# Attention with a score product for the row maxima and a second one with keys on partitions, in place of transposed probabilities

## The chip, the cores and the metric

The kernel runs on one core of one Trainium2 chip. The metric is the device time of one execution in microseconds (us). The core's engines run side by side and wait for each other by semaphores: TensorE (PE; PEld is its loading of weights), VectorE (DVE), ScalarE (ACT), GpSimd (POOL), and SyncE (SP), which issues most transfers.

## What is computed

One program holds two blocks over 512 latent tokens of width 1024 and 256 context tokens. The first block (retention, neighbourhood and memory attention, a mixture of experts) is untouched by the change. The second block is two transformer layers, each with modulation, an attention of three kinds, and a gated feed-forward part. The attention of every head is

```
def _sdpa(q, k, v, scale):
    s = einsum('qd,kd->qk', q, k) * scale
    p = softmax(s, axis=-1)
    return einsum('qk,kd->qd', p, v)
```

in float32. A layer has 20 heads: 4 latent heads (query and key width 96), 8 differential ones (width 32, in four pairs whose outputs are subtracted and normalized), and 8 grouped ones (width 64; four heads share keys and values). Values are 64 wide. In layer 0 the 512 latent queries see all 768 keys, and the 256 context queries see the 256 context keys; in layer 1 only the latent queries are needed.

## The kernel before, in words

Numbers that need float32 accuracy go through TensorE as float32r, each as a high and a low part that add up (`split`, line 88: ScalarE rounds the high part, VectorE subtracts). Queries and keys of a latent head are split in two, and a score is three products of 96 rows: high by high, high by low, low by high. A differential head stacks its parts on 96 rows and needs one product. A grouped head stacks the query's two parts over twice the key's high part (128 rows, `k1`) and adds the query's high part by the key's low part (64 rows, `k2`).

`pipeline` (line 1867) runs over the 20 heads. For each head, `scores` (line 1888) takes the query tiles of 128 one by one: the products fill a PSUM tile of 128 queries by 768 keys (`sn`, line 1899; two such tiles exist, of two banks each), VectorE takes the negated maximum of each row (line 1905), ScalarE writes the exponentials `pn` with the maximum as bias and sums the rows on the way (line 1908). The two context tiles share one tile (lines 1913, 1919); line 1921 takes the reciprocals of the sums (`srec`).

`turned` (line 1924) then brings the keys onto partitions: per part of 128 keys by 512 queries (in layer 0 also one of 2 x 128 keys by 256 context queries) four float32 transposes `tp` on TensorE (line 131), and a split: by ScalarE from PSUM and VectorE (line 92), or, for the parts marked in `SPLITS` (line 1864), a copy by ScalarE (line 1940), a cast by VectorE (line 1941), and a subtraction on GpSimd (line 1942). `products` (line 1948) multiplies them with the values: the values, high and low side by side (`vp`, 128 columns), are the weights, and the 512 probabilities move past, high part and low part in turn (line 1957). ScalarE copies the result `oT` (line 1961), `fold` (line 1966) turns it back and adds the two halves by one float32 product per query tile (line 1970), and VectorE multiplies with the reciprocal into the merged rows `yB` (line 2001; line 1817 for the differential heads).

The order is written out in the loop of `pipeline`: a step of head u's `turned`, the products of parts that are more than `LAG` = 5 behind (line 1984), a step of head u+1's `scores`, and one step of preparing head u+2 (line 1992): its rows are loaded, split on VectorE and GpSimd (`dqst`, `gqst`), and turned by float32r transposes (line 129). Of PSUM's eight banks the two score tiles take four, `tp` three, `pv` one (line 1238). After the last head the merged rows are transposed (`trp`) for the output projection.

Of the kernel before, what the change touches and what calls it, by code (L numbers as in the profile page):

```python
# [23 lines left out]
# columns of the vector pack, in blocks of 128 features  # L24
# [8 lines left out]
# groups of 256 columns of the second block's input projection: name, first column  # L33
# [4 lines left out]
class Kern:  # L38
# [15 lines left out]
    def W(self, ap, n=2048, k=None, steps=1, pin=False, eng=None):  # L54
        """Weight chunk [128, n] of float32 from DRAM as an exact pair of float32r tiles."""
        key = ap.tensor.name, ap.offset
        if key in self.early:
            return self.early.pop(key)
        return self.pair(self.raw(ap, n), n, k, steps, pin, eng)

    def ahead(self, *chunks):
        """Loads weight chunks (name, index, k) before their use; W finds them then."""
        for name, at, k in chunks:
            ap = self.i[name][at]
            key = ap.tensor.name, ap.offset
            self.early[key] = self.W(ap, k=k)
# [6 lines left out]
    def pair(self, raw, n=2048, k=None, steps=1, pin=False, eng=None):  # L73
        """pin: not before what the engines have to do first, though it may seem ready."""
# [12 lines left out]
    def split(self, hi, lo, src, scale=None, bias=None):  # L87
        """hi + lo = src (times scale), both float32r."""
# [15 lines left out]
    def psum(self, mm, big=0, words=1024, own=()):  # L104
        """Banks of PSUM: mm of one bank, big of several."""
# [16 lines left out]
    def rows6(self, name, dtype=F):  # L122
        """[128, 6, 1024]: six tiles of rows, or what else takes their place."""
# [53 lines left out]
    def transpose_rows(self, rows, nt, dst, evac):  # L177
        """rows: list of [128, 1024] tiles; evac(kt, t0, n, psum [128, n*128])."""
# [25 lines left out]
    # =====================================================================  # L204
# [70 lines left out]
    def first_norm(self, t):  # L275
        """Norms the row tiles from t on that share a step: 0, 1, or 2 and 3."""
# [41 lines left out]
    def proj_a(self, g, evac):  # L318
        """Columns on partitions: out[128 columns, 512 tokens]."""
# [17 lines left out]
    def retention(self):  # L337
# [6 lines left out]
        y = rp.tile([128, 4, 1024], F, name="y")              # [tok, tile, 4 heads of 256]  # L344
# [3 lines left out]
        def queries(c):  # L348
            """q and k of the heads 2c, 2c + 1: [128, hi or lo, head, tok]"""
# [34 lines left out]
        def scores(hd):  # L384
            # decay by the distance of the tokens: E[p, i - 128 j + 384] for tile j of the keys
# [15 lines left out]
        def outputs(hd):  # L401
# [4 lines left out]
            for i in range(4):  # L406
# [6 lines left out]
                # group norm over the head's 256 values  # L413
# [9 lines left out]
        # log sigmoid of the decays: min(x, 0) - log1p(exp(-|x|)), log1p by its atanh series  # L423
# [41 lines left out]
        # silu of the gate projection  # L465
# [64 lines left out]
        # per query column qq of a tile, the 32 columns of its key window, for the three tile types  # L530
        # (window starts 16, 8 and 0 columns before the tile): [qq, qr, h, type, 256]
# [6 lines left out]
    def neighbourhood(self):  # L538
# [19 lines left out]
        starts = (256, 192, 64, 0)               # key windows of the query tiles 3, 2, 1, 0  # L558
# [42 lines left out]
    def exps(self, out, s, m, scale):  # L601
        """out = exp(scale * (s - max)) for two tiles of queries [128, 2, 256]; returns 1 / row sums."""
# [47 lines left out]
    def memory_rows(self):  # L650
        """Normed rows of the memory."""
# [14 lines left out]
    def memory_keys(self, rows):  # L666
        """Keys and values of the memory."""
# [63 lines left out]
    def b1_out(self, *stages):  # L731
        """stages: what follows for each tile of rows; the sums of squares of its parts are in self.xss."""
# [39 lines left out]
    # =====================================================================  # L772
    def moe(self):
# [21 lines left out]
        # normed rows, to DRAM for the gathers and transposed for the router  # L795
# [37 lines left out]
        # group: maximum of the softmax, first one on ties  # L833
# [1418 lines left out]
```

## Time and profile before

| | |
|---|---|
| three runs | 3068.51, 3056.35, 3059.96 us, median 3059.96 |
| profiled execution | span 3055.9 us, so the median lies 4.1 us above it |
| TensorE busy | 95% of the span |
| its weight loads | 81% |
| VectorE, ScalarE, GpSimd busy | 58%, 42%, 16% |
| attention of layer 0 | about 1258 to 1548 us of the span |
| attention of layer 1 | about 2364 to 2607 us |

Matmuls are pipelined, so the time that one shows is longer than the distance from its start to the next one's; what a product costs in a row of others is read from starts. A group "x4" in a timeline is four instructions on end. Where a float32 product with a narrow moving side runs, the trace holds two records for it.

### The profile page before, as it was taken

How to read it: one execution, taken by the hardware profiler on the slowest of the kernel's cores; microseconds unless marked ns; L12 is line 12 of the kernel's file. 1: busy time of each engine (PE TensorE's matmuls, PEld its weight loads, DVE VectorE, ACT ScalarE, POOL GpSimd, SP SyncE). 2: the span in 40 equal slices, each digit the busy share in tenths (PEclk: the TensorE clock that was granted, in tenths of full speed). 3: DMA queues.
4: the chain of work that ended last, by engine and by line, in shares of the span. 5: the costliest groups of instructions: out<-in, count | busy, mean ns of one | idle time of the engine just before them, and what ended most of it. 6: DMA issues, size and time to landing. Idle time of an engine off the chain costs nothing. (4 is left out here: it accounts for less than half of the span.)

```text
span 3055.9 us, 44719 instructions
## 1 busy us (share of the span) xinstructions
PE 2907.7 (95%) x17896; PEld 2473.1 (81%) x17896; DVE 1784.5 (58%) x3187; ACT 1296.3 (42%) x2275; POOL 483.3 (16%) x478
## 2 busy tenths in 40 slices
PE   8999999999899979899998999999898999899998
PEld 6997777679788869787688888888798776788887
DVE  6652254346688876788747242434665886644445
ACT  3232243324577754597645121211342876432222
POOL 2200010001110042255312000000310543100001
PEclk9999999999899989999999999999999999899999
DMA  5443464446799862510023121212143300322221
GB/s 197 153 140 138 143 234 152 183 155 242 267 392 378 312 225 75 179 27 19 1 90 128 59 71 54 78 48 83 62 138 98 96 20 1 125 110 96 97 97 69
DMA packets 130084, 399.78 MB, mean 131 GB/s; under 512 B 62199, under 2 KB 74887, under 8 KB 93128
## 3 DMA queue, kind: packets, MB, share of 16 engines
q1 hardware_dynamic: 116206, 350.04, 31.9%
q0 software_dynamic: 13520, 46.55, 4.6%
q8 instruction: 143, 2.34, 0.3%
q14 instruction: 71, 0.58, 0.1%
q10 hardware_dynamic: 144, 0.26, 0.0%
HBM read 356.64 MB, written 39.39 MB: 130 GB/s over the span
## 5 line engine op out<-in xcount | busy, mean ns | idle before, releaser
L82 DVE TENSOR_TENSOR wlo<-raw,whi 128x2048 fp32r<-128x2048 f32 (+2 forms) x195 | 419.3, 2153 | 280.2 <-ACT whi L81 279.7
L81 ACT ACTIVATE whi<-raw 128x2048 fp32r<-128x2048 f32 (+2 forms) x203 | 351.9, 1739 | 490.9 <-PE fd L101 132.2
L99 PE MATMUL fg<-hT,whi 128*128 128x512 f32 (+1 forms) x1120 | 389.1, 348 | 2.1 <-ACT hT L1374 2.1
L100 PE MATMUL fg<-hT,whi 128*128 128x512 f32 (+1 forms) x1120 | 389.7, 348 | 1.2 <-POOL hT L1376 1.2
L101 PE MATMUL fg<-hT,wlo 128*128 128x512 f32 (+1 forms) x1120 | 389.2, 348 | 0.0
L100 PEld LDWEIGHTS fg<-hT,whi 128*128 128x128 f32 x1120 | 213.7, 191 | 31.0 <-POOL hT L1376 1.7
L99 PEld LDWEIGHTS fg<-hT,whi 128*128 128x128 f32 x1120 | 212.1, 190 | 31.9 <-ACT hT L1374 2.5
L101 PEld LDWEIGHTS fg<-hT,wlo 128*128 128x128 f32 x1120 | 212.0, 189 | 29.0
L1942 POOL TENSOR_TENSOR pelo<-pe,pehi 128x512 fp32r<-128x512 f32 x140 | 180.7, 1292 | 233.5 <-DVE pehi L1941 227.1
L2104 DVE TENSOR_TENSOR sg<-sg,fg 128x512 f32<-128x512 f32 (+1 forms) x70 | 40.1, 572 | 295.0 <-PE fg L101 295.0
L101 PE MATMUL fd<-whi,hl 128*128 128x512 f32 x440 | 174.9, 397 | 0.0
L1905 DVE TENSOR_REDUCE smx<-sn 128x1 f32<-128x768 f32 x160 | 152.3, 952 | 38.2 <-PE sn L1899 37.7
L100 PE MATMUL fd<-wlo,hh 128*128 128x512 f32 x440 | 174.6, 397 | 0.0
L99 PE MATMUL fd<-whi,hh 128*128 128x512 f32 x440 | 174.1, 396 | 0.0
L2080 POOL TENSOR_TENSOR acc<-acc,gt 128x512 f32<-128x512 f32 x20 | 30.7, 1536 | 867.9 <-ACT sqj L164 867.9
L2075 DVE TENSOR_TENSOR acc<-acc,fd 128x512 f32<-128x512 f32 x180 | 120.7, 685 | 71.9 <-PE fd L101 71.9
L131 PE MATMUL tp<-ident,pn 128*128 128x128 f32 x960 | 151.8, 278 | 2.6 <-DVE pelo L92 1.8
L1908 ACT ACTIVATE pn<-sn,smx 128x768 f32<-128x768 f32 x160 | 143.5, 902 | 12.0 <-DVE smx L1905 6.8
L99 PE MATMUL eg<-whi,xt 128*96 128x256 f32 x512 | 146.5, 286 | 0.0
L100 PE MATMUL eg<-wlo,xt 128*96 128x256 f32 x512 | 144.6, 282 | 0.9 <-DVE wlo L82 0.9
L82 DVE TENSOR_TENSOR wlo<-rawx,whi 128x2048 fp32r<-128x2048 f32 x58 | 132.9, 2292 | 20.9 <-ACT whi L81 20.8
L101 PE MATMUL eg<-whi,xt 128*96 128x256 f32 x512 | 144.3, 282 | 0.0
(661 smaller groups left out, 7755.8 us busy)
## 6 DMA issues: line engine op xcount, KB each, us to landing
raw<-in_w_in SPq DMA_DIRECT2D x53, 1024.0 KB, 5.0
raw<-in_w_ada SPq DMA_DIRECT2D x48, 1024.0 KB, 5.1
raw<-in_f_gate SPq DMA_DIRECT2D x22, 1024.0 KB, 4.8
raw<-in_f_up SPq DMA_DIRECT2D x22, 1024.0 KB, 4.8
raw<-in_f_down SPq DMA_DIRECT2D x22, 1024.0 KB, 4.8
rawx<-in_e_gate SPq DMA_DIRECT2D x19, 1024.0 KB, 14.2
rawx<-in_e_up SPq DMA_DIRECT2D x19, 1024.0 KB, 8.9
rawx<-in_e_down SPq DMA_DIRECT2D x18, 1024.0 KB, 8.3
```

Of the source, the lines that this page charges most:

```text
L81: keep(nc.scalar.activation(hi[:, c], raw[:, c], AF.Copy))
L82: keep((eng or nc.vector).tensor_tensor(lo[:, c], raw[:, c], hi[:, c].bitcast(F), op=OP.subtract))
L99: t.matmul(ps, lh, rh, start=first, stop=False)
L100: t.matmul(ps, lh, rl, start=False, stop=False)
L101: t.matmul(ps, ll, rh, start=False, stop=last)
L131: self.nc.tensor.transpose(out, in_, self.ident[:k, :k])
L1905: nc.vector.tensor_reduce(m[:, t:t + 1], p[:, :768], axis=AX.X, op=OP.max, negate=True)
L1908: nc.scalar.activation(P[t], p[:, :768], AF.Exp, bias=m[:, t:t + 1], accum_out=su[:, t:t + 1])
L1942: nc.gpsimd.tensor_tensor(el, e, eh.bitcast(F), op=OP.subtract)
L2075: nc.vector.tensor_tensor(acc[:, t, cs], acc[:, t, cs], p, op=OP.add)
L2080: nc.gpsimd.tensor_tensor(acc[:, t, cs], acc[:, t, cs], gt[t // 4][:, cs], op=OP.mult)
L2104: nc.vector.tensor_tensor(sg, sg, pp[1], op=OP.mult)
```

## The change

Each head now has two score products. `maxima` (in place of `scores`) makes a first one, with queries on partitions and with the first pass alone (high by high for latent heads, all of it for differential ones, the 128-row pass for grouped ones); VectorE writes the negated row maxima into a column of a padded tile `mz`, small products with the identity turn that tile, and ScalarE copies the one row of maxima under the queries' rows (`late`). The keys get a row of ones at the same place, so that `exps` can make a second product, with keys on partitions and 256 queries moving, from which the maxima are already subtracted: 97 rows in place of 96, and 65 in place of 64. ScalarE's exponential of it is already in the layout that the product with the values wants. It is used as it is, in float32, for parts 2 and 5 of the differential and grouped heads (`plain`), and otherwise split: the high part by ScalarE or VectorE (`HIGH`), the low part on GpSimd.

In `products` the probabilities are now the weights (128 x 128), and the values move: 130 columns of [low, high, ones] for the high part, 66 of [high, ones] for the low part. Query tiles come out on partitions and the column of ones gives the sums, so `turned`, the accumulating of sums in the exponential, and `fold` go. Each pair of query tiles ends by a reciprocal, a copy, an addition, and a multiplication that moves from VectorE to GpSimd. There is one score tile for the maxima in place of two, two banks each are for `st`, `pv` and `tp`, and `LAG` is 4. A few memsets on GpSimd write the ones, and a copy on VectorE makes the second query tile of grouped heads.

```diff
-                with self.pool("l_at") as ap, self.psum(1, 2, own=dict(pv=1, tp=3)):
+                with self.pool("l_at") as ap, self.psum(1, 1, own=dict(st=2, pv=2, tp=2)):
...
-        nc.vector.tensor_copy(v[:, :, :64], r)
-        nc.gpsimd.tensor_tensor(v[:, :, 64:], r, v[:, :, :64].bitcast(F), op=OP.subtract)
-        return v
+        nc.vector.tensor_copy(v[:, :, 64:128], r[:, :, :64])
+        nc.gpsimd.tensor_tensor(v[:, :, :64], r[:, :, :64], v[:, :, 64:128].bitcast(F), op=OP.subtract)
+        nc.gpsimd.memset(v[:, :, 128:130].bitcast(F), 1.0)
+        nc.gpsimd.memset(r[:, :, 64:66], 1.0)
+        return v, r
...
-        return [(hi[0], hi[1], 96), (hi[0], lo[1], 96), (lo[0], hi[1], 96)], v
+        return dict(first=(hi[0], hi[1], 96), row=96, late=hi[0], v=v, plain=(),
+                    passes=[(hi[1], hi[0], 97), (lo[1], hi[0], 96), (hi[1], lo[0], 96)])
...
-            return [(q, k, 96)], v
+            return dict(first=(q, k, 96), row=96, late=q, passes=[(k, q, 97)], v=v, plain=(2, 5))
...
-            return [(q1, T1, 128), (q1, T2, 64)], v
+            return dict(first=(q1, T1, 128), row=64, late=q2, passes=[(T1, q1, 128), (T2, q2, 65)], v=v, plain=(2, 5))
...
-    SPLITS = (1, 0, 1, 0, 1, 0, 1)
-    LAG = 5
+    HIGH = (1, 0, 0, 1, 0, 0, 1)
+    LAG = 4
...
-        groups = [(0, 4, 0)] + ([(4, 2, 4)] if nq > 4 else [])
+        groups = [(0, 0, 6), (2, 0, 6)] + ([(4, 4, 6)] if nq > 4 else [])
...
+        def maxima(u):
...
             for t in range(4):
                 p = self.big("sn")
-                mms(p[:, :512], t, 0, 512)
-                mms(p[:, 512:768], t, 512, 768)
-                nc.vector.tensor_reduce(m[:, t:t + 1], p[:, :768], axis=AX.X, op=OP.max, negate=True)
-                P[t] = ap.tile([128, 768], F, name="pn", bufs=6)
+                qs = slice(t * 128, t * 128 + 128)
+                for a, b in ((0, 512), (512, 768)):
+                    nc.tensor.matmul(p[:, a:b], q[:rows, qs], k[:rows, a:b], start=True, stop=True)
+                nc.vector.tensor_reduce(mz[:, t, row:row + 1], p[:, :768], axis=AX.X, op=OP.max, negate=True)
                 yield
-                nc.scalar.activation(P[t], p[:, :768], AF.Exp, bias=m[:, t:t + 1], accum_out=su[:, t:t + 1])
...
+            for t0 in range(0, nq, 4):
+                n = min(4, nq - t0)
+                p = self.mm("tp")
+                for t in range(n):
+                    nc.tensor.matmul(p[:row + 1, t * 128:t * 128 + 128], mz[:, t0 + t, :row + 1], self.identr, start=True, stop=True)
+                nc.scalar.activation(late[row:row + 1, t0 * 128:(t0 + n) * 128], p[row:row + 1, :n * 128], AF.Copy)
+                yield
+        def exps(u):
...
+                    for a in range(2):
+                        ks = slice((k + a) * 128, (k + a) * 128 + 128)
+                        for j, (kT, qT, rows) in enumerate(passes):
+                            nc.tensor.matmul(p[:, a * 256:a * 256 + 256], kT[:rows, ks], qT[:rows, qs], start=j == 0,
+                                             stop=j == len(passes) - 1)
+                    if i in plain:
+                        e, eh, el = ap.tile([128, 512], F, name="pf", bufs=3), None, None
+                        nc.scalar.activation(e, p, AF.Exp)
                     else:
-                        self.split(eh, el, p)
+                        e = ap.tile([128, 512], F, name="pe", bufs=4)
+                        nc.scalar.activation(e, p, AF.Exp)
+                        eh, el = self.pairs8[0]
+                        self.pairs8.append(self.pairs8.pop(0))
+                        if self.HIGH[i]:
+                            nc.scalar.activation(eh, e, AF.Copy)
+                        else:
+                            nc.vector.tensor_scalar(eh, e, 1.0, None, op0=OP.mult)
+                        nc.gpsimd.tensor_tensor(el, e, eh.bitcast(F), op=OP.subtract)
...
             if k == k0:
                 self.pv = self.mm("pv")
-            p = self.pv[:, :N]
-            for a in range(512 // N):
-                for e in (eh, el):
-                    nc.tensor.matmul(p, v[:, k + a], e[:, a * N:a * N + N], start=k == k0 and a == 0 and e is eh,
-                                     stop=k + a == 5 and e is el)
...
+                    if eh is None:
+                        add(pv[:, t, 64:130], e[:, c], vf[:, k + a, :66], first, last)
+                    else:
+                        add(pv[:, t], eh[:, c], v[:, k + a], first, False)
+                        add(pv[:, t, 64:130], el[:, c], v[:, k + a, 64:130], False, last)
+            if k + 2 < k1:
                 return
-            folds.append([1, u, o, rec])
...
+            rec = self.small.tile([128, 2, 1], F, name="srec")
+            nc.vector.reciprocal(rec, pv[:, :, 128:129])
+            o = ap.tile([128, 2, 64], F, name="oS", bufs=3)
+            nc.scalar.activation(o, pv[:, :, :64], AF.Copy)
+            nc.vector.tensor_tensor(o, o, pv[:, :, 64:128], op=OP.add)
+            units[u][1](t0, rec.to_broadcast([128, 2, 64]), o)
...
     def scaled(self, yB, c, nq):
-        def ev(rec, p):
-            self.nc.vector.tensor_tensor(yB[:, :nq, c:c + 64], p, rec, op=OP.mult)
+        def ev(t0, rec, o):
+            self.nc.gpsimd.tensor_tensor(yB[:, t0:t0 + 2, c:c + 64], o, rec, op=OP.mult)
```

On TensorE, a stretch among the grouped heads of layer 0 stands so in the program before (`sn` are score tiles, `gkT` and `gqT` turned keys and queries, `tp` transposes, `pn` exponentials, `pv` the products with the values, `pehi` and `pelo` the split probabilities; behind the arrow the operands, with the moving shape):

```order
L1899 MATMUL sn<-gkT_14252,gqT_14710 128x512
L1899 MATMUL sn<-gkT_14295,gqT_14710 128x512
L1899 MATMUL sn<-gkT_14252,gqT_14710 128x256
L1899 MATMUL sn<-gkT_14295,gqT_14710 128x256
L129 MATMUL tp<-identr,gk_14838 128x128 x4
L131 MATMUL tp<-ident,pn 128x128 x4
L1957 MATMUL pv<-pehi,vp 128x512
L1957 MATMUL pv<-pelo,vp 128x512
```

And so, at the like place, in the changed program (`st` are scores with keys on partitions; the tile 15319 is the low part of the next group's keys):

```order
L1919 MATMUL sn<-gkT_14617,gqT_15159 128x512
L1919 MATMUL sn<-gkT_14617,gqT_15159 128x256
L129 MATMUL tp<-identr,gk_15319 65x128 x4
L1947 MATMUL st<-gqT_14979,gkT_14617 128x256
L1947 MATMUL st<-gqT_14978,gkT_14676 128x256
L1947 MATMUL st<-gqT_14979,gkT_14617 128x256
L1947 MATMUL st<-gqT_14978,gkT_14676 128x256
L1975 MATMUL pv<-vp,pehi 128x130
L1975 MATMUL pv<-vp,pelo 128x66
L1975 MATMUL pv<-vp,pehi 128x130
L1975 MATMUL pv<-vp,pelo 128x66
```

The second pass of the scores left the product for the maxima, the transposes of `pn` gave way to scores, and two wide products with the values became eight narrow ones per part (two pairs of them are shown).

On GpSimd, at the start of the grouped heads, the program before has (`gqst` is the split of a query, `vp` that of the values):

```order
L1840 TENSOR_TENSOR gqst<-gqr,gqst 128x6x64
L1942 TENSOR_TENSOR pelo<-pe,pehi 128x512 x3
L1840 TENSOR_TENSOR gqst<-gqr,gqst 128x6x64
L1942 TENSOR_TENSOR pelo<-pe,pehi 128x512
L1840 TENSOR_TENSOR gqst<-gqr,gqst 128x6x64
L1721 TENSOR_TENSOR vp<-vr,vp 128x6x64
```

The changed program has there (`yB` are merged rows, `oS` the output before its scaling, `do` the second output of a differential pair):

```order
L1838 TENSOR_TENSOR do_14558<-yB 128x384
L1860 TENSOR_TENSOR gqst<-gqr,gqst 128x6x64
L1829 TENSOR_TENSOR yB<-oS,srec 128x2x64
L1961 TENSOR_TENSOR pelo<-pe,pehi 128x512
L1860 TENSOR_TENSOR gqst<-gqr,gqst 128x6x64
L1961 TENSOR_TENSOR pelo<-pe,pehi 128x512 x2
L1829 TENSOR_TENSOR yB<-oS,srec 128x2x64
L1961 TENSOR_TENSOR pelo<-pe,pehi 128x512
```

The scaling of the outputs came in between GpSimd's subtractions, and there are more of these: 196 in both layers, where 140 stood.

## Rows read from the trace of the kernel before

**Rows 1.** Windows, latent/differential/grouped heads, layers 0, 1: us, busy (count), clock, DMA, GB/s:

```profile
1272.25:1313.12 40.87, 37.78 (x261) 33.03 (x260) 33.27 (x58) 33.34 (x77) 21.28 (x19) 1.00 0.41 121
1313.12:1407.57 94.45, 88.03 (x627) 75.49 (x626) 85.91 (x138) 85.83 (x202) 57.91 (x53) 1.00 0.12 26
1407.57:1532.72 125.15, 124.33 (x670) 87.21 (x669) 90.14 (x150) 82.28 (x189) 48.73 (x40) 1.00 0.03 6
2376.68:2409.90 33.22, 30.99 (x201) 25.74 (x199) 29.35 (x50) 26.87 (x57) 18.66 (x16) 1.00 0.45 141
2409.90:2488.17 78.27, 75.31 (x505) 60.10 (x503) 70.36 (x124) 69.24 (x148) 45.43 (x46) 1.00 0.13 29
2488.17:2593.04 104.87, 102.09 (x523) 69.29 (x522) 71.45 (x128) 65.52 (x132) 36.10 (x31) 1.00 0.02 5
```

**Rows 2.** Timeline, VectorE: a reciprocal ends each score stage (start, us, engine, what):

```profile
1407.57 0.18 DVE L1921 RECIPROCAL srec<-ssum 128x6 f32<-128x6 f32 x1
...
1532.72 0.19 DVE L1921 RECIPROCAL srec<-ssum 128x6 f32<-128x6 f32 x1 [0.48 <-ACT pc L1919]
```

**Rows 3.** Timeline, TensorE, a grouped head: score weight loads; score products and what follows:

```profile
1466.24 1.13 PEld L1899 LDWEIGHTS sn<-gkT,gqT 128*128 128x128 f32 x4
...
1473.03 1.44 PE L1899 MATMUL sn<-gkT,gqT 128*128 128x512 f32 x4
1474.40 0.54 PE L129 MATMUL tp<-identr,gqst 128*128 128x128 f32 x4
```

**Rows 4.** Timeline, TensorE, a differential head: score products, transposes:

```profile
1337.12 0.52 PE L1899 MATMUL sn<-dkT,dqT 96*128 96x512 f32 x2
1337.48 0.42 PE L129 MATMUL tp<-identr,dqst 128*96 128x128 f32 x4
1337.73 0.62 PE L131 MATMUL tp<-ident,pn 128*128 128x128 f32 x4
```

**Rows 5.** Timeline, TensorE: fold products and their weight loads; loads of float32r transposes:

```profile
1343.35 0.97 PEld L1970 LDWEIGHTS tp<-fold,oT 128*128 128x128 f32 x8
1343.45 1.00 PE L1970 MATMUL tp<-fold,oT 128*128 128x64 f32 x8
...
1474.40 0.40 PEld L129 LDWEIGHTS tp<-identr,gqst 128*128 128x128 f32 x4
```

**Rows 6.** Timeline, TensorE: first and last of six products with the values:

```profile
1539.88 0.39 PE L1957 MATMUL pv<-pehi,vp 128*128 128x512 f32 x1
...
1541.02 0.40 PE L1957 MATMUL pv<-pelo,vp 128*128 128x512 f32 x1
```

**Rows 7.** Groups by form, TensorE, whole run (count, busy us, mean ns, idle before):

```profile
L131 PE MATMUL tp<-ident,pn 128*128 128x128 f32 x960 | 151.8, 278 | 2.6 <-DVE pelo L92 1.8
L1970 PE MATMUL tp<-fold,oT 128*128 128x64 f32 x400 | 52.4, 269 | 4.0 <-ACT oT L1961 3.7 <-DVE pelo L92 0.3
```

**Rows 8.** Groups by form, attention of layer 0: GpSimd, VectorE, ScalarE:

```profile
L1942 POOL TENSOR_TENSOR pelo<-pe,pehi 128x512 fp32r<-128x512 f32 x80 | 103.6, 1297 | 130.7 <-DVE pehi L1941 128.1 <-DVE dif_y L151 2.5
L1804 POOL TENSOR_TENSOR dqst<-dqrow,dqst 128x192 fp32r<-128x192 f32 x8 | 6.8, 851 | 0.3 <-DVE dqst L1803 0.3
L1905 DVE TENSOR_REDUCE smx<-sn 128x1 f32<-128x768 f32 x80 | 76.0, 951 | 15.3 <-PE sn L1899 15.0
L1940 ACT ACTIVATE pe<-tp 128x512 f32<-128x512 f32 x80 | 47.8, 597 | 23.4 <-PE tp L131 22.3
```

**Rows 9.** Line 1941, the cast on VectorE (min/median/max ns); one cast beside GpSimd:

```profile
L1941 DVE CAST pehi<-pe x140: 385/426/1503, 1270.9 to 2597.6; 128x512 fp32r<-128x512 f32 x140
...
1337.80 2.65 POOL L1942 TENSOR_TENSOR pelo<-pe,pehi 128x512 fp32r<-128x512 f32 x2 [2.71 <-DVE pehi L1941]
...
1339.43 1.30 DVE L1941 CAST pehi<-pe 128x512 fp32r<-128x512 f32 x1
```

**Rows 10.** Timeline, TensorE: the first product after the attention of either layer:

```profile
1547.81 0.47 PE L131 MATMUL trp<-ident,yB 128*128 128x128 f32 x1 [1.86 <-DVE yB L2001]
...
2606.91 1.33 PE L131 MATMUL trp<-ident,yB 128*128 128x128 f32 x5 [1.44 <-DVE yB L2001]
```

More of the change, by code (lines that the diff above doesn't have):

```diff
@@ L1734, in to_T @@
             nc.scalar.activation(o[:n, c], p[:n, :m * 128], AF.Copy)
+            if again is not None:
+                nc.vector.tensor_copy(again[:64, c], p[:64, :m * 128])
             yield
@@ L1771, in attention @@
             self.pairs8 += [(hi[:, j], lo[:, j]) for j in range(4)]
-        raw = self.wp.tile([128, 4, 512], F, name="pe", tag="raw", bufs=self.NRAW)
-        self.copies = [raw[:, j] for j in range(4)]
-        self.fold = ap.tile([128, 64], F, name="fold")
-        nc.vector.tensor_tensor(self.fold, self.ident[:, :64], self.ident[:, 64:], op=OP.add)
+        self.negmax = {}
+        for row in (96, 64):
+            self.negmax[row] = ap.tile([128, 6, row + 2], R, name="mz%d" % row)
+            nc.gpsimd.memset(self.negmax[row].bitcast(F), 0.0)
         units = []
@@ L1886, in prepare @@
                 steps = steps and steps - 1
-        def scores(u):
+        def maxima(u):
             prepare(u, None)
-            passes = ready[u][0]
-            m = self.small.tile([128, 6], F, name="smx")
-            su = self.small.tile([128, 6], F, name="ssum")
-            P = {}
-            def mms(p, t, a, b):
-                qs = slice(t * 128, t * 128 + 128)
-                for j, (q, k, rows) in enumerate(passes):
-                    nc.tensor.matmul(p, q[:rows, qs], k[:rows, a:b], start=j == 0, stop=j == len(passes) - 1)
+            q, k, rows = ready[u]["first"]
+            row, late = ready[u]["row"], ready[u]["late"]
+            mz = self.negmax[row]
             for t in range(4):
                 p = self.big("sn")
-                mms(p[:, :512], t, 0, 512)
-                mms(p[:, 512:768], t, 512, 768)
-                nc.vector.tensor_reduce(m[:, t:t + 1], p[:, :768], axis=AX.X, op=OP.max, negate=True)
-                P[t] = ap.tile([128, 768], F, name="pn", bufs=6)
+                qs = slice(t * 128, t * 128 + 128)
+                for a, b in ((0, 512), (512, 768)):
+                    nc.tensor.matmul(p[:, a:b], q[:rows, qs], k[:rows, a:b], start=True, stop=True)
+                nc.vector.tensor_reduce(mz[:, t, row:row + 1], p[:, :768], axis=AX.X, op=OP.max, negate=True)
                 yield
-                nc.scalar.activation(P[t], p[:, :768], AF.Exp, bias=m[:, t:t + 1], accum_out=su[:, t:t + 1])
             if nq > 4:
@@ L1911, in scores @@
                 for a in range(2):
-                    mms(p[:, a], 4 + a, 512, 768)
-                nc.vector.tensor_reduce(m[:, 4:6], p, axis=AX.X, op=OP.max, negate=True)
-                pc = ap.tile([128, 2, 256], F, name="pc", bufs=2)
+                    nc.tensor.matmul(p[:, a], q[:rows, 512 + a * 128:640 + a * 128], k[:rows, 512:768], start=True, stop=True)
+                nc.vector.tensor_reduce(mz[:, 4:6, row], p, axis=AX.X, op=OP.max, negate=True)
                 yield
-                for a in range(2):
-                    t = 4 + a
-                    P[t] = pc[:, a]
-                    nc.scalar.activation(P[t], p[:, a], AF.Exp, bias=m[:, t:t + 1], accum_out=su[:, t:t + 1])
@@ new lines, in exps @@
+        def exps(u):
+            i = 0
+            passes, plain = ready[u]["passes"], ready[u]["plain"]
+            for t0, k0, k1 in groups:
+                qs = slice(t0 * 128, t0 * 128 + 256)
+                for k in range(k0, k1, 2):
+                    p = self.mm("st")
+                    for a in range(2):
[15 more added lines that the diff above has]
+                            nc.vector.tensor_scalar(eh, e, 1.0, None, op0=OP.mult)
@@ L1962, in products @@
-            if t0 + N // 128 < nq:
-                return
-            folds.append([1, u, o, rec])
-        def fold():
-            _, u, o, rec = folds.pop(0)
-            pf = self.mm("tp")[:, :nq * 64].rearrange("p (t d) -> p t d", t=nq)
-            for t in range(nq):
-                nc.tensor.matmul(pf[:, t], o[:, t * 128:t * 128 + 128], self.fold, start=True, stop=True)
-            units[u][1](rec[:, :nq].to_broadcast([128, nq, 64]), pf)
+            pv = self.pv[:, :260].rearrange("p (t n) -> p t n", t=2)
@@ new lines, in add @@
+            def add(o, lhs, rhs, first, last):
+                nc.tensor.matmul(o, lhs, rhs, start=first, stop=last, skip_group_check=True)
+            for a in range(2):
+                for t in range(2):
+                    c = slice(a * 256 + t * 128, a * 256 + t * 128 + 128)
+                    first, last = k == k0 and a == 0 and t == 0, k + 2 == k1 and a == 1
+                    if eh is None:
+                        add(pv[:, t, 64:130], e[:, c], vf[:, k + a, :66], first, last)
+                    else:
+                        add(pv[:, t], eh[:, c], v[:, k + a], first, False)
+                        add(pv[:, t, 64:130], el[:, c], v[:, k + a, 64:130], False, last)
@@ L1973, in step @@
+            if k + 2 < k1:
+                return
+            rec = self.small.tile([128, 2, 1], F, name="srec")
[4 more added lines that the diff above has]
+            units[u][1](t0, rec.to_broadcast([128, 2, 64]), o)
         def step(g):
             return next(g, self) is not self
-        for _ in scores(0):
+        for _ in maxima(0):
@@ L1977, in pipeline @@
             prepare(1, 1)
         for u in range(len(units)):
-            B = turned(u)
-            A = scores(u + 1) if u + 1 < len(units) else None
+            B = exps(u)
+            A = maxima(u + 1) if u + 1 < len(units) else None
             while A or B:
@@ L1987, in pipeline @@
                     A = None
-                if folds:
-                    folds[0][0] -= 1
-                    if folds[0][0] < 0:
-                        fold()
                 prepare(u + 2, 1)
@@ L1994, in pipeline, with ev @@
             products()
-        while folds:
-            fold()
     def scaled(self, yB, c, nq):
-        def ev(rec, p):
-            self.nc.vector.tensor_tensor(yB[:, :nq, c:c + 64], p, rec, op=OP.mult)
+        def ev(t0, rec, o):
+            self.nc.gpsimd.tensor_tensor(yB[:, t0:t0 + 2, c:c + 64], o, rec, op=OP.mult)
         return ev
```

104 lines of the change are left out of this document (47 added, 57 removed).

## The prediction

> **What bounds the kernel now.** I read the busy shares first (TensorE 95%), then busy time by stretch of the two attentions, then TensorE's own timeline inside one head. The stretches were cut at the reciprocals that end a head's scores [rows 2]. In [rows 1] the columns behind the stretch's length are TensorE, its weight loads, VectorE, ScalarE, GpSimd, granted clock, share of DMA. The clock is 1.00 throughout (its upper level, 2.4 GHz), so times can be compared across stretches. In the grouped heads TensorE is busy 124.33 of 125.15 us in layer 0 and 102.09 of 104.87 in layer 1: only its own instructions count there. Latent heads stand at 37.78 of 40.87 and 30.99 of 33.22 with DMA at 0.41 to 0.45, differential ones at 88.03 of 94.45 and 75.31 of 78.27, where VectorE and ScalarE are at 90%. A grouped head takes 125.15 / 8 = 15.6 us in layer 0 and 13.1 in layer 1, a differential one 11.8 and 9.8, a latent one 40.87 / 3 = 13.6 and 11.1. With 4, 8 and 8 heads per layer, TensorE's instructions per head are what the change is priced by.
>
> **Spacings.** What a product costs is the distance of starts. 512 moving columns: (1541.02 - 1539.88) / 5 = 0.228 us [rows 6], so 256 take 0.115 by half. A pair of 512 and 256 columns on 96 rows: 1337.48 - 1337.12 = 0.36 [rows 4]. The four score products of a grouped query tile: 1474.40 - 1473.03 = 1.37, with 1.13 / 4 = 0.28 for one load of weights [rows 3]; twice two pairs of 0.36 would be 0.72, so alternating 128 with 64 rows costs 0.65 more per query tile. A float32 transpose: (0.62 - 0.278) / 3 = 0.114 [rows 4, 7], a load of fold's 0.97 / 8 = 0.121 against (1.00 - 0.269) / 7 = 0.104 between fold records [rows 5, 7]; I take 0.11 for both, and the trace has two records per fold product.
>
> **The change, TensorE, one head.** Removed in layer 0 (layer 1): 28 (24) transposes, 3.08 (2.64); 12 products with the values of 512 columns and 4 (0) of 256, 3.20 (2.74); 12 (8) fold records, 1.32 (0.88). Together 7.60 (6.26). Also removed are the scores: grouped 4 x 1.37 and four (0) of 256 columns at 0.31, a little under 1.37 / 4, 6.73 (5.48); latent three passes of 1.67 (1.44), a pass being 4 x 0.36 + 2 (0) x 0.115; differential one.
>
> Added: the product for the maxima, one pass, 1.67 (1.44). The second product, 14 (12) times 256 columns per pass, 1.61 (1.38); two passes for grouped heads, three for latent, one for differential. The small products with `mz`, 6 (4) at 0.09, 0.54 (0.36). And the products with the values: 56 (48) records of probabilities as weights, since a split part has 4 of 130 columns and 4 of 66, and a plain float32 part 4 products of two records. No row shows a narrow float32r product that isn't a transpose. The nearest that is a product is fold's, also with 64 columns past a fresh load of 128 x 128: I take its 0.11 and get 6.16 (5.28). The ends are 0.08 (between the float32r transposes of [rows 4], 0.25 / 4 = 0.063, and their loads, 0.40 / 4 = 0.10 [rows 5]) and 0.222, if such a product takes two records as fold's do.
>
> The grouped head: 14.33 out, 11.59 in, -2.74 (11.74 and 9.84, -1.90); times 8 -21.9 - 15.2 = -37. This rests on the 65-row pass not paying what the 64-row pass pays. The latent head: 12.61 out, 13.20 in, +0.6 in both layers, times 8 +5. The differential head: 9.27 out, 9.98 in, +0.7; but TensorE idles 0.8 us of each of these in layer 0 and 0.4 in layer 1 [rows 1], and four vector operations per part (copy, cast or subtraction, maximum, exponential) lose the copy from PSUM, so most of it goes into that idle time. Between 0 and +11 for 16 heads, I take +4.
>
> **What lies beside.** ScalarE loses the copies, 0.597 each [rows 8], and gets a few small ones: hidden by TensorE in all heads. One score tile in place of two: the next maxima product waits for VectorE's 0.951 [rows 8]. In the loop it has a step of 4 score products and 8 with the values between (some 1.3 us), which covers it where VectorE comes at once; queued behind a held product are the next part's products and, through them, ScalarE's exponential. I take 0.3 us on each of the 24 latent and grouped heads, +7; the ends are 0 and 0.95 on six maxima of each, +137, which I count as unlikely since VectorE is at 72% in grouped heads and loses its second subtraction per part. The memsets, the transfers by SP and the copy `q2` have no waiter that is on time; nothing is moved past SP's or POOL's queues but the scalings below.
>
> **The tails.** From the last reciprocal to the first transpose after it pass 1547.81 - 1532.72 = 15.1 us and 2606.91 - 2593.04 = 13.9 [rows 1, 2, 10]. There the last head turns, splits, multiplies and folds. Afterwards it has 3.22 + 6.16 of second scores and products, and about 2 for the last exponential, split, addition and scaling: 11.5 and, with 2.76 + 5.28, 10.0. -3.6 - 3.9 = -7.5.
>
> **Sum.** -37 + 5 + 4 + 7 - 7.5 = -28 on the profiled span of 3055.9, 3028; the runs' median lies 4.1 above the span, so 3032.
>
> **Rivals.**
>
> A. The narrow products stream as tightly as the float32r transposes do: 0.08 in place of 0.11. On the latent and grouped heads, which TensorE bounds, 8 x (40 + 32) + 4 x (56 + 48) = 992 records are narrow float32r, times 0.030 = -30: 3002. For it: no float32 double pass, a load of 0.10. Against: fold's records, whose moving side is half as wide, don't get there. The Trainium skill (TensorE: Matmul & The Clock Gate, Back-to-back issue gap) gives 81 ns as the sustained spacing of load and matmul pairs with 128 columns; by it this rival's sum is the one. The fold rows of this case stand above that figure, the transposes about at it.
>
> B. GpSimd becomes the bound. Its subtraction takes 1.297 us, one of 192 elements 0.851 [rows 8]; 128 by the slope of these two is 0.76. Per differential head of layer 0: 5 x 1.297, 2 x 0.851, 3 scalings at 0.76, half of a square and of a value split at 1.1: 11.6, where the head has 11.8; a latent head 7 x 1.297 + 2.3 + 1.1 = 12.5 of 13.6. In [rows 1] it needs 57.91 of 94.45. And it holds VectorE: a cast beside it took 1.30 (at 1339.43, inside the subtractions from 1337.80), where the median is 0.426 [rows 9]. If the subtractions are late by as much as the added scalings (2.3 us) in a third of the heads, +2.3 x 13 = +30 less what LAG covers, the gain is gone: about 3055. For it: the sum of 11.6 against 11.8. Against: in the grouped heads, where most of the gain is, it needs some 10 of 13. The Trainium skill (GPSIMD Engine Reference, 8. Key points) says that GpSimd shares its SBUF interfaces with VectorE and is contended for by operations with two SBUF inputs; that speaks against moving the scalings to it, and the cast of 1.30 agrees.
>
> C, on the slow side: the 65-row pass still alternates with the 128-row one at a price. If each of its 28 (24) products per grouped head pays the exposed 0.195 (0.31 less 0.115), the second product costs 8 x (5.5 + 4.7) = +81: 3113. It decides from 28 / 416 = 0.067 per product. Against: 96-row products stand beside 128-row ones without a gap [rows 4]. For: no row has 65 rows, and the 64-row ones pay.
>
> D, also slow: narrow float32r products take two records as float32 ones do. +0.11 on the 1568 of them is +172: 3204; break-even is at 28 / 1568 more, 0.128. For: every narrow product of the trace is float32 and does. Against: transposes in float32r show one record.
>
> **The numbers.** Forecast 0.45, A 0.25, B 0.15, C 0.07, D 0.08. A measurement tells 0.5% from no change, 3044.7 and 3075.3. The forecast's own range is 3015 to 3055 by the stalls and the differential heads: faster 0.34 of its 0.45, the rest the same; A is faster nearly always; B is the same for 0.09, slower 0.02, faster 0.04; C and D are slower. Faster 0.62, same 0.20, slower 0.18. The range goes from 2990, a little below A, to 3080, and leaves out C and D.
>
> **What would show it.** Right: grouped heads at about 13.0 and 11.3 us with TensorE still at 98%; latent heads 0.7 longer; starts of products with the values 0.11 apart; 65-row products at 0.115; the tail at 11.5. Wrong: spacings of 0.08 (A); a chain of waits through GpSimd's subtractions, or casts at 1.3 in most parts (B); score loads of 0.28 at the second product (C); two records for `pv` in float32r (D); TensorE idle before `sn`, released by VectorE's maximum, would break the term of the single score tile.

## The result: 10.7% slower, the attentions at half the clock

The changed kernel takes 3384.16 us (median of four runs, 3375.93 to 3396.88) against 3063.87 before: a ratio of 1.107, 95% interval 1.1034 to 1.1106. The forecast was 3032. The page of its profile differs in one row above all, the granted clock; the digits are tenths, in 40 slices of the span:

```profile
span 3378.9 us, 46615 instructions
PE 3233.2 (96%) x18824; PEld 2895.4 (86%) x18824; DVE 1722.0 (51%) x3157; ACT 1247.3 (37%) x2075; POOL 606.4 (18%) x714
PEclk8999989998999895555579999999896555689999
```

The kernel before:

```profile
PEclk9999999999899989999999999999999999899999
```

The two runs of fives are the two attentions. In windows cut at the reciprocals that end a kind's last head (three latent heads, eight differential, eight grouped, then layer 1; columns as in [rows 1]; in the changed kernel this reciprocal ends the head's last product with the values, in [rows 1] it ends the head's scores):

```profile
1312.76:1389.87 77.11, 77.11 (x363) 75.85 (x364) 27.05 (x53) 30.12 (x59) 34.13 (x42) 0.50 0.08 22
1389.87:1557.50 167.63, 167.63 (x793) 164.38 (x794) 69.11 (x135) 76.25 (x152) 78.97 (x99) 0.50 0.07 16
1557.50:1727.50 170.00, 169.99 (x804) 167.41 (x804) 64.93 (x137) 66.82 (x128) 63.51 (x68) 0.50 0.03 8
2579.60:2643.80 64.20, 64.20 (x299) 62.98 (x300) 23.15 (x45) 22.64 (x43) 29.17 (x36) 0.50 0.09 27
2643.80:2785.40 141.60, 141.60 (x665) 138.43 (x665) 58.25 (x107) 59.35 (x112) 64.57 (x83) 0.50 0.07 15
2785.40:2928.60 143.20, 143.14 (x670) 140.53 (x670) 53.41 (x105) 52.11 (x92) 50.42 (x51) 0.50 0.02 8
```

[rows 1] had 1.00 in that column throughout. TensorE is busy all the time, as the profile counts it, and VectorE, ScalarE and GpSimd less than half: TensorE is the bound, at its lower level (0.50 of 2.4 GHz is 1.2 GHz). From the first score product to the first product behind the attention, layer 0 takes 465.6 us (290.0 before) and layer 1 388.4 (242.2): +175.6 and +146.2 of the 323.0 by which the span grew. The stretches before, between and behind the attentions changed by +8.5, -6.0 and -1.3.

How the clock was lost, in windows of the changed kernel:

```profile
1290.00:1300.00 10.00, 9.99 (x87) 9.74 (x85) 9.64 (x14) 8.25 (x14) 9.94 (x12) 1.00 0.35 78
1300.00:1303.00 3.00, 1.04 (x9) 0.89 (x8) 2.21 (x3) 0.00 (x0) 3.00 (x3) 0.98 0.00 0
1303.00:1310.00 7.00, 4.99 (x23) 4.73 (x22) 3.41 (x6) 2.83 (x7) 3.93 (x5) 0.50 0.52 178
1310.00:1727.00 417.00, 417.00 (x1971) 410.04 (x1970) 162.08 (x327) 174.65 (x341) 177.63 (x209) 0.50 0.06 14
```

And TensorE's timeline there. A part has eight narrow products with the values, four pairs of 130 and 66 columns; shown are the first of the eight and what follows the last, at either clock:

```profile
1297.37 0.23 PE L1975 MATMUL pv<-vp,pehi 128*128 128x130 f32 x1
...
1298.19 0.59 PE L1919 MATMUL sn<-mhi 96*128 96x512 f32 x2
...
1302.27 0.61 PE L1919 MATMUL sn<-mhi 96*128 96x512 f32 x2 [1.96 <-DVE mz L1920]
...
1593.45 0.31 PE L1975 MATMUL pv<-vp,pehi 128*128 128x130 f32 x1
...
1595.01 0.99 PE L1919 MATMUL sn<-gkT,gqT 128*128 128x512 f32 x2
```

For ten microseconds the new mixture runs at 1.00, and the eight products of a part take 1298.19 - 1297.37 = 0.82 us (0.81 in most parts), 0.10 each. Then TensorE waits 1.96 us for a maximum, since there is one score tile; the clock falls, and 417 us of unbroken work don't bring it back. The eight now take 1595.01 - 1593.45 = 1.56. The kernel before idled as well (3.04 us for a transfer, up to 1263.18 us), fell, and came back:

```profile
1264.30:1267.80 3.50, 3.50 (x15) 3.15 (x14) 2.47 (x5) 1.58 (x4) 1.00 (x1) 0.51 1.01 248
1267.80:1272.00 4.20, 4.06 (x30) 3.33 (x29) 3.36 (x6) 3.43 (x10) 0.55 (x1) 1.00 0.53 127
```

### The profile page after: what moved, and what is told of

Its sections match the earlier page's. It is cut to its first block, busy times and chain, and to the rows that moved or that the text cites. A ratio compares the mean times of both kernels' runs of the same rounds, so it can differ in the third digit from the quotient of the medians.

```text
span 3378.9 us, 46615 instructions
## 1 busy us (share of the span) xinstructions
PE 3233.2 (96%) x18824; PEld 2895.4 (86%) x18824; DVE 1722.0 (51%) x3157; ACT 1247.3 (37%) x2075; POOL 606.4 (18%) x714
## 5 line engine op out<-in xcount | busy, mean ns | idle before, releaser
L1975 PE MATMUL pv<-vp,pehi 128*128 128x130 f32 x784 | 306.5, 414 | 0.0
L1961 POOL TENSOR_TENSOR pelo<-pe,pehi 128x512 fp32r<-128x512 f32 x196 | 255.1, 1302 | 252.8 <-ACT pehi L1958 114.7
L1975 PE MATMUL pv<-vp,pelo 128*128 128x66 f32 x784 | 279.0, 357 | 0.5 <-POOL pelo L1961 0.5
L1975 PEld LDWEIGHTS pv<-vp,pelo 128*128 128x128 f32 x784 | 255.9, 326 | 1.0 <-POOL pelo L1961 0.9
L1975 PEld LDWEIGHTS pv<-vp,pehi 128*128 128x128 f32 x784 | 255.6, 326 | 0.0
L1920 DVE TENSOR_REDUCE mz<-sn 128x1 fp32r<-128x768 f32 x160 | 152.9, 956 | 185.4 <-PE sn L1919 166.6
L1954 ACT ACTIVATE pe<-st 128x512 f32<-128x512 f32 x196 | 117.0, 597 | 181.6 <-PE st L1947 175.4
L99 PE MATMUL eg<-whi,xt 128*96 128x256 f32 x512 | 146.5, 286 | 0.0
```

The source lines that it names most:

```text
L99: t.matmul(ps, lh, rh, start=first, stop=False)
L1920: nc.vector.tensor_reduce(mz[:, t, row:row + 1], p[:, :768], axis=AX.X, op=OP.max, negate=True)
L1954: nc.scalar.activation(e, p, AF.Exp)
L1961: nc.gpsimd.tensor_tensor(el, e, eh.bitcast(F), op=OP.subtract)
L1975: nc.tensor.matmul(o, lhs, rhs, start=first, stop=last, skip_group_check=True)
```

## The experiments

Theory N: narrow products, each behind a weight load of its own, keep the clock down. Rivals: idle gaps alone (G), or the number of weight loads (W).

**Wider products with the values, all else as changed.** The 130 or 66 columns that move run on into the next key tile's values (the tile of values is one key tile longer for it), and the extra columns land in PSUM columns that nobody reads.

```diff
...
-                        add(pv[:, t], eh[:, c], v[:, k + a], first, False)
-                        add(pv[:, t, 64:130], el[:, c], v[:, k + a, 64:130], False, last)
+                        at = (k + a) * 130
+                        add(pv[:, t], eh[:, c], vw[:, at:at + 256], first, False)
+                        add(pv[:, t, 64:256], el[:, c], vw[:, at + 64:at + 256], False, last)
```

> The changed kernel, in which the split products with the values move 256 and 192 columns in place of 130 and 66 (the further columns are the next key tile's values, land in unused PSUM columns and are ignored). At the upper clock a product of 256 columns has 0.115 us against 0.11, so the added columns should cost some 5 us in all. Theory N (narrow products behind their weight loads keep the granted clock at 0.50): the clock stands at 1.00 in most of both attentions, 424 + 360 us at 0.50 shrink to half, and the time is about 3000 us (2970 to 3040). Rival G (idle gaps of TensorE at the start of each attention bring the clock down, whatever the products' width): the gaps stay, the clock stays at 0.50, 3380 us. Rival W (weight loads, as many as before, are what matters): 0.50, 3380 us.

Measured 3089.79 us, ratio to before 1.0096 (1.0068 to 1.0123): 294 us less than the changed kernel, for more columns, though above the 2970 to 3040 that N gave. The number of weight loads is the same, they are busy for the same share of TensorE's time (95.33 of 97.36 us in the last window below, 410.04 of 417.00 in the changed kernel), and the stalls are still there. Its windows, cut as above, without layer 1:

```profile
1307.00:1354.10 47.10, 43.15 (x363) 42.07 (x362) 26.34 (x53) 29.29 (x60) 33.85 (x43) 1.00 0.14 39
1354.10:1464.40 110.30, 102.03 (x793) 97.20 (x793) 71.16 (x135) 72.74 (x153) 80.85 (x104) 0.94 0.11 24
1464.40:1569.10 104.70, 97.36 (x804) 95.33 (x803) 68.81 (x138) 65.33 (x129) 65.33 (x69) 0.95 0.03 6
```

And around its longest stall, in steps of 10 us:

```profile
1470.00:1480.00 10.00, 2.90 (x24) 2.68 (x23) 9.58 (x27) 2.36 (x5) 3.28 (x3) 0.84 0.01 2
1480.00:1490.00 10.00, 10.00 (x57) 9.76 (x58) 6.61 (x15) 4.06 (x9) 5.13 (x7) 0.64 0.05 3
1490.00:1500.00 10.00, 10.00 (x89) 9.83 (x89) 5.32 (x11) 7.55 (x15) 6.08 (x8) 1.00 0.01 2
```

The wider products are not free at the upper clock: eight take 1470.79 - 1469.89 = 0.90 us (lines below), 0.09 more than the narrow ones, some 18 us over 196 parts. So N holds in this form: after each fall behind a stall from 1300 us on the wide mixture is back at 1.00 within some 10 us, where the changed kernel, once it had fallen behind a stall with the narrow products running, did not come back in either attention. G and W alone fall.

**A burst of 32 wide products ahead of head 10.** The first product of its second scores, over 512 columns, 32 times into a tile that isn't read.

```diff
+            if u == 10:
+                kT, qT, rows = ready[u]["passes"][0]
+                p = self.mm("tp")
+                for _ in range(32):
+                    nc.tensor.matmul(p, kT[:rows, :128], qT[:rows, :512], start=True, stop=True)
             B = exps(u)
```

> The changed kernel with 32 more products of 512 columns before head 10 of each layer, whose result is not used: 32 x 0.43 = 14 us at the lower clock, 7 at the upper. They should raise the clock. Theory N: with the narrow products after them the clock falls back to 0.50 without an idle gap; the time is 3380 + 15 to 25 us. Rival G (an idle gap is needed for a fall): the clock stands at 1.00 from head 10 to the end of each attention, which halves some 210 + 180 us: about 3200 us.

Measured 3392.83 us (1.1079, 1.1028 to 1.1129), where N said 3395 to 3405. The windows of layer 0 around it:

```profile
1500.00:1508.00 8.00, 8.00 (x40) 8.00 (x41) 1.84 (x6) 3.10 (x8) 2.79 (x3) 0.50 0.01 2
1508.00:1512.00 4.00, 4.00 (x12) 3.10 (x12) 0.29 (x1) 0.86 (x2) 1.64 (x2) 0.60 0.20 45
1512.00:1529.00 17.00, 16.31 (x122) 15.08 (x121) 9.21 (x14) 8.08 (x16) 8.54 (x11) 1.00 0.10 24
1529.00:1532.00 3.00, 0.77 (x9) 0.66 (x7) 1.19 (x4) 1.22 (x4) 2.07 (x3) 0.94 0.00 0
1532.00:1732.00 200.00, 200.00 (x945) 196.86 (x945) 79.87 (x162) 80.78 (x154) 76.97 (x83) 0.50 0.03 9
```

The burst raises the clock, and the narrow mixture holds it for 13 us behind the burst; it is lost at the next stall (0.77 busy of 3.00) and not regained in 200 us. Here the fall did need a stall, against the expectation from N.

**Two score tiles**, with one bank each for the products with the values and for transposes.

```diff
-                with self.pool("l_at") as ap, self.psum(1, 1, own=dict(st=2, pv=2, tp=2)):
+                with self.pool("l_at") as ap, self.psum(1, 2, own=dict(st=2, pv=1, tp=1)):
```

> The changed kernel with two score tiles for the maxima, as before the change, and one bank each for the products with the values and the transposes in place of two. It shortens the idle gaps of TensorE that wait for VectorE's maximum at the start of each attention (1.96 us at 1300 us of the span). Rival G: with the gaps gone the clock stays at 1.00, about 3000 us. Theory N: the clock falls all the same, and the time stays within 3350 to 3420 us.

Measured 3313.13 us (1.0818, 1.0758 to 1.0879), lower than N's band and far above G's. Two of its windows, one in each layer:

```profile
1326.00:1580.00 254.00, 253.11 (x1183) 247.22 (x1183) 107.10 (x216) 105.84 (x216) 115.39 (x142) 0.50 0.06 13
2797.00:2856.00 59.00, 56.05 (x464) 53.73 (x463) 31.96 (x57) 36.06 (x69) 33.17 (x34) 1.00 0.01 1
```

The same grouped mixture runs at either level. The fall at 1324 had no stall longer than 0.22 us in the 4 us before it:

```profile
1323.75 0.33 PE L1975 MATMUL pv<-vp,pehi 128*128 128x130 f32 x1 [0.22 <-DVE oS L1992]
```

And here the narrow mixture did regain the clock, once in the middle of unbroken work:

```profile
1599.00:1600.00 1.00, 1.00 (x7) 1.00 (x6) 0.94 (x2) 0.38 (x1) 0.00 (x0) 0.50 0.00 0
1600.00:1601.00 1.00, 1.00 (x9) 0.90 (x8) 0.32 (x3) 0.65 (x2) 0.40 (x1) 0.64 0.00 0
1601.00:1602.00 1.00, 1.00 (x12) 1.00 (x10) 1.00 (x2) 1.00 (x2) 0.29 (x1) 1.00 0.02 8
```

From 1594.24 to this rise TensorE ran score products, transposes and one plain part, and none of the split products of 130 and 66 columns; the rises at 1580, 1662, 2751 and 2795 us came behind such stretches too, of 5 to 7 us, after 14 to 256 us at the lower level. A like stretch of 5.8 us in the changed kernel (1595.01 to 1600.78) brought none. So the narrow mixture stands close to where the clock is lost or regained, and small things decide.

**Only the high part wide** (256 columns), the low part at 66.

```diff
...
-                        add(pv[:, t], eh[:, c], v[:, k + a], first, False)
+                        at = (k + a) * 130
+                        add(pv[:, t], eh[:, c], vw[:, at:at + 256], first, False)
                         add(pv[:, t, 64:130], el[:, c], v[:, k + a, 64:130], False, last)
```

> The changed kernel in which the high part's products move 256 columns and the low part's stay at 66. If the clock follows the columns that move, this lies between the changed kernel (about 3380) and the wide one (3090): the clock comes back after a stall, but later, and the time is 3090 to 3200 us. If it were only the low part's 66 columns that keep the clock down, it stays at 3380.

Measured 3217.67 us (1.0525, 1.0466 to 1.0584), a little above the band expected, at a mean clock of 0.912 between 0.855 and 0.963: graded. Behind a stall this mixture did come back, but late: it stood at 0.50 from 1349 to 1500, from 1519 to 1592 and from 2523 to 2681 us.

**The kernel before, its products cut narrow.** No second scores, no row of maxima, two score tiles.

```diff
-                    nc.tensor.matmul(p, v[:, k + a], e[:, a * N:a * N + N], start=k == k0 and a == 0 and e is eh,
-                                     stop=k + a == 5 and e is el)
+                    for c in range(0, N, 128):
+                        nc.tensor.matmul(p[:, c:c + 128], v[:, k + a], e[:, a * N + c:a * N + c + 128],
...
```

> The kernel before the change, in which each product with the values of 512 (256) columns is cut in four (two) of 128 columns with the same weights, loaded anew each time: 56 and 48 products a head at 0.11 us in place of 3.20 and 2.74 us, +3.0 and +2.5 us on 20 heads each, 3170 us at the upper clock. Theory N in its strict form (narrow products keep the clock down wherever they stand): the clock falls at the first idle stretch of each attention and stays at 0.50, which adds 300 us or more: 3450 to 3800 us. If it takes what else the change does (the narrow products of the row of maxima, the waits for one score tile) to lose the clock, 3160 to 3200 us with the clock near 1.00.

Measured 3258.05 us (1.0647, 1.0596 to 1.0698), between the two expectations. Windows in the grouped heads of layer 0:

```profile
1472.00:1480.00 8.00, 7.76 (x48) 5.87 (x48) 3.35 (x5) 4.81 (x10) 3.19 (x3) 1.00 0.11 25
1480.00:1540.00 60.00, 60.00 (x231) 48.52 (x230) 27.82 (x57) 18.95 (x41) 11.79 (x10) 0.50 0.01 1
```

```profile
1478.32 1.32 PE L1899 MATMUL sn<-gkT,gqT 128*128 128x256 f32 x4 [0.22 <-ACT pn L1908]
```

The longest idle time in these 8 us before the fall is 0.22 us, and the clock was lost all the same, for all but some 3 us of the rest of that attention. In the grouped heads of layer 1 it held, as the page's row shows:

```profile
PEclk8999999998999999995559999999999999989999
```

Narrow products behind a load each can thus lose the clock, without anything else of the change, but not everywhere.

**What is left once the clock is mostly back.** The wide kernel is still 1% slower than before. One place in it, TensorE first, then VectorE:

```profile
1469.89 0.28 PE L1977 MATMUL pv<-vp,pehi 128*128 128x256 f32 x1
...
1470.79 0.53 PE L1920 MATMUL sn<-gkT,gqT 128*128 128x512 f32 x2
1471.16 0.64 PE L1948 MATMUL st<-gqT,gkT 128*128 128x256 f32 x4
1471.64 0.28 PE L1977 MATMUL pv<-vp,pehi 128*128 128x256 f32 x1
...
1479.80 1.01 PE L1920 MATMUL sn<-gkT,gqT 128*128 128x512 f32 x2 [7.10 <-DVE mz L1921]
```

```profile
1470.22 1.14 DVE L150 TENSOR_SCALAR dif_y<-dif_v 128x24 int32<-128x24 int32 x1
...
1476.72 1.82 DVE L1882 TENSOR_TENSOR yB<-yB,gdiff 128x256 f32<-128x256 f32 x2
...
1478.80 0.94 DVE L1921 TENSOR_REDUCE mz<-sn 128x1 fp32r<-128x768 f32 x1
```

VectorE works through the normalization of the differential heads; a maximum stands queued behind it, and with one score tile TensorE stands 7.10 us. From 1290 and 2390 us on, waits for maxima add up to 19 and 14 us in the two layers, most of it in these rows (total, times, longest):

```profile
PE sn L1920 <- DVE mz L1921: 16.0, 10, 7.1
...
PE sn L1920 <- DVE mz L1921: 13.9, 6, 4.8
```

Behind the longest of them the wide kernel falls to the lower clock as well. Two more runs give it two score tiles:

> The changed kernel with both edits: products with the values over 256 and 192 columns, and two score tiles for the maxima (one bank each then for the products with the values and for transposes). The wide kernel waited 16.0 + 13.9 us for the maximum of the one score tile and fell to the lower clock behind the longest of these waits. If these waits are what is left of the loss, the two tiles take away most of 30 us and some 15 us of lower clock: about 3045 to 3055 us, less what the single bank for the products with the values costs (9.4 us of waits in layer 0 when it was tried with narrow products): 3055. If the rest of the loss is TensorE's own instructions, the time stays at 3090.

Measured 3127.09 us (1.0239, 1.0204 to 1.0273): slower than the wide kernel, not the 3055 expected. The waits for the maximum went in layer 0, but those of the products with the values for the addition that frees their one bank came to 31.2 us there (total, times, longest):

```profile
PE pv L1977 <- DVE oS L1995: 31.2, 22, 4.1
```

With `own=dict(st=1, pv=2, tp=1)`:

> As the last one, with two banks for the products with the values and one for the second scores. The waits for the addition behind a single such bank (9.4 us in layer 0) go; a part's second scores must wait for the exponential of the part before (0.6 us on ScalarE), which eight products with the values cover (1 us). About 3040 us, under the kernel before; if the exponential isn't covered, 0.5 us on 260 parts, 3170.

Measured 3076.63 us (1.0065, 1.0040 to 1.0090), the best version with the change's structure, but not the 3040 expected. The normalization is still waited for, now through ScalarE: its copy at 1460.52 us had waited 4.84 us for a reciprocal queued on VectorE behind the normalization, and the next exponential stood behind that copy (total, times, longest):

```profile
PE st L1948 <- ACT pe L1955: 9.1, 8, 4.8
```

**The differential heads' scalings and squares back on VectorE**, in that version.

```diff
-                    nc.gpsimd.tensor_tensor(y[:, t0:t0 + 2], o, rec, op=OP.mult)
+                    nc.vector.tensor_tensor(y[:, t0:t0 + 2], o, rec, op=OP.mult)
...
```

> The wide kernel with two score tiles and two banks for the products with the values, and the scalings and the squares of the differential heads back on VectorE, where they were before the change. If VectorE's waits for GpSimd at the end of each pair (1.65 us for the scaling, 0.71 for the square at 1423 us of the span, behind which a maximum is late and TensorE idles 2.4 us) cost time, the time falls by 5 to 20 us, to 3055 to 3070 beside 3077. If VectorE's own time takes the place of the wait, it is the same.

Measured 3076.90 us: no difference from 3076.63. Having moved these to GpSimd wasn't what cost the time.

**The 64-row pass alone, in the kernel before.**

```diff
-                k2 = ap.tile([128, 6, 64], R, name="gk2", tag="st", bufs=3)
+                k2 = ap.tile([128, 6, 96], R, name="gk2", tag="st", bufs=3)
+                nc.gpsimd.memset(k2[:, :, 64:].bitcast(F), 0.0)
...
-            return [(q1, T1, 128), (q1, T2, 64)], v
+            return [(q1, T1, 128), (q1, T2, 96)], v
```

> The kernel before the change, with one edit: the second pass of a grouped head's scores runs on 96 rows (32 of them zeros on the key's side) in place of 64. If the 0.65 us that a query tile pays in the kernel before is the price of alternating 128-row with 64-row products, the grouped heads lose 3.3 us in layer 0 and 2.9 in layer 1, -49 us over 16 heads: about 3010 us, and this part of the change's gain could be had without the rest. If the price comes from alternating two sets of keys at all, the time stays at 3060.

Measured 3015.71 us, ratio 0.9861 (0.9822 to 0.9900): 1.4% faster than the kernel before, near the 3010 expected. The four score products of a query tile take 1442.54 - 1441.83 = 0.71 us, where [rows 3] gave 1.37:

```profile
1441.83 0.88 PE L1900 MATMUL sn<-gkT,gqT 128*128 128x512 f32 x4
1442.54 0.46 PE L129 MATMUL tp<-identr,gqst 128*128 128x128 f32 x4
```

The attentions take 270.5 and 222.7 us, 19.5 less each.

## Why the prediction was wrong

**The step that failed** is the sentence "The clock is 1.00 throughout (its upper level, 2.4 GHz), so times can be compared across stretches". It was true of [rows 1] and was carried over to a mixture that had never run. Every duration in the sum is one at the upper clock; the sum prices a product by its distance in time alone, by which 130 columns behind a load cost little less than 256. That another mixture might not hold the clock had no term, and none of the rivals A to D had the clock in it. What the runs showed in its place: 0.50 in all six windows of the two attentions. The wider products, which bring most of the clock back and cost some 18 us of their own, took 294 of the 320 us away. The Trainium skill (TensorE: Matmul & The Clock Gate, What's actually happening) says that throttled is the default state and activity releases it; that should have made a rival. This case differs from that rule of the Trainium skill: 417.00 of 417.00 us busy, at 0.50.

**The sizes at the upper clock.** Narrow products 0.10 us apart (0.81 / 8), a little under the 0.11 of the forecast, so neither A (0.08) nor D (0.222). Four products of a second score in 1471.64 - 1471.16 = 0.48 us, 0.12 each, 65 rows among them, so not C. B was not it: GpSimd is at 47% at most in the windows of the changed kernel and at 73% in those of the wide one (80.85 of 110.30), TensorE waited for its subtractions 1.6 and 1.3 us in the wide kernel's attentions, and giving work back to VectorE changed nothing. The slow cast of [rows 9] reads one tile, so it is no case of two inputs; in the wide kernel the cast's median is 0.61 us. The end of +137 for the single score tile counted six maxima a head; a head has five in layer 0 and four in layer 1, which makes it 103.

**The sum, read from the wide kernel**, whose attentions are 19.7 and 4.5 us longer than before where the terms gave -28 together. The eight grouped heads take 104.7 us against 125.15 in [rows 1], -20.5 (forecast -21.9), and 86.7 against 104.87 in layer 1, -18.2 (-15.2). That these windows come so near is partly luck: the first holds the wait of 7.10 us and the lower clock behind it, and the last head of either has no maxima of a next one beside it (8.07 and 7.77 us). Between the ends of two undisturbed grouped heads pass 12.35 and 10.41 us (to 1538.22 and 2599.96 us), before the change 15.48 and 12.93 (to 1517.77 and 2580.43): -3.1 and -2.5 a head, where the forecast had -2.74 and -1.90. Three latent heads lost 6.2 and 5.5 (forecast 2 each), the differential 15.9 and 5.9 (4 together), some of it at the lower clock (0.94 in layer 0): the term for the one score tile was 7 and measured as waits 19 and 14 us. And the term for the tails was -7.5, but it left out the beginning: from the first score to the first cut, and from the last cut on, pass 43.2 + 4.4 us in layer 0 where 14.4 + 15.1 stood; since the cuts lie later in a head now, only the sums compare, 47.6 against 29.5. The first head's maxima go one at a time through one tile, then through `mz`, with nothing beside them, and the clock is at 0.50 for 24 us of it.

**Where the gain came from.** The kernel before with 96 rows in the second pass gains 19.5 us in each attention, and its undisturbed grouped heads take 12.14 and 10.34 us (to 1507.04 and 2531.37 us), about what the wide kernel's take. So, by these times, the change's only gain is that its second scores have no 64-row pass, and removing the transposes of probabilities paid for the second scores and the narrower products, and no more. This is read from equal times; no run put a 64-row pass into the changed kernel.

What stays open: what exactly the mixture must have for the clock to return. In one run the narrow mixture stood at 0.50 for 254 us in layer 0, and its grouped heads ran at 1.00 for 59 us in layer 1.

## What to carry to other kernels

Before trading wide products for narrow ones behind fresh weights, ask what the clock will do; a stretch at 100% busy and 0.50 is slower than one at 90% and 1.00, and padding the moving side to 256 and 192 columns, which costs 0.09 us a part at the upper clock here, gave back 294 us in all. When PSUM is shared out anew, name for each tile the slowest instruction that can stand ahead of its reader, not the reader's own time. And split off the cheap part of a change: 32 rows of zeros gained 1.4%, and no version with the rest of the change was faster than the kernel before.

## What the runs showed of the hardware that was not expected

- More moving columns made the kernel faster: 1568 products widened to 256 and 192 columns, eight of them 0.90 us in place of 0.81 at the upper clock, and the mean clock from 0.855 to 0.963.
- TensorE stayed at the lower clock through 417 us without a pause, and the same instructions ran at the upper one elsewhere (59 us with two score tiles). The clock fell twice with no idle time over 0.22 us just before.
- Score products of 128 rows alternating with 64 rows cost 1.37 us a query tile, with 96 rows 0.71, the 32 rows of zeros included.
